# Feed-forward: early output products cut in three and written between the seven block products, TensorE in written order there, first such pair one later

## The chip, the cores and the metric

The kernel runs on one core of one Trainium2 chip. The metric is the device time of one execution in microseconds (us). Five engines matter here: TensorE (PE in the profile, with its weight loads as PEld), VectorE (DVE), ScalarE (ACT), GpSimd (POOL) and SyncE (SP), which only issues DMAs. Each engine works through its own instructions in one fixed order, and an instruction waits for semaphores that others raise.

## The reference

Two layers, each a feed-forward block, a mixer (neighbourhood attention in the first, a bidirectional RWKV-7 in the second) and another feed-forward block, with a normalized residual after each: four feed-forward blocks in all. Only they are touched:

```
D_MODEL, SEQ, D_FF = 1024, 512, 2816

def swiglu(x, w_in, w_out):
    gate, up = jnp.split(x @ w_in, 2, axis=-1)
    return (jax.nn.silu(gate) * up) @ w_out
...
x = layer_norm(DN_ALPHA * x + 0.5 * swiglu(x, ffn_w_in[i, 0], ffn_w_out[i, 0]), ln_g[i, 0], ln_b[i, 0])
```

x has 512 tokens of 1024 channels, w_in 1024 x 5632 and w_out 2816 x 1024, all float32.

## The kernel before

**Numbers.** A float32 operand is held as two parts: a rounded high part, made by an activation on ACT (line 277), and the remainder, a subtraction on DVE (line 278). This pair of steps is called a split. A product of two such operands is three matmuls: high by high, high by low, low by high.

**Blocks.** The 2816 hidden channels are 22 blocks f of 128, taken as 11 pairs c (f = 2c and f = 2c + 1) in `ffn` (line 462). A *standard block* (`proj`, line 291) takes gate and up one after the other: 2 x 8 x 3 = 48 matmuls of 512 columns (lines 287 to 289). Gate goes to one PSUM bank and up to another. ACT takes the silu of gate (line 494) and DVE multiplies it with up (line 496). From f = 2 on, `Seven.banks` gives every block the same two banks, so a block can't start in a bank before the last block's readers are done with it.

**Seven products.** The odd blocks from f = 3 on (`SEVEN`, line 83) use a 2 x 2 block scheme with seven multiplications in place of eight (`Seven.products`, line 962). Each product is 12 matmuls of 256 columns (line 979), 84 in all. Names used below: a, f, e, a2, e2, f2, e3, in the written order of the seven calls of `mul`. a and f (and a2, f2) share the first bank, e, e2 and e3 have the second. After a, ACT copies it from the first bank into the second, `copy(e, a)` (line 985 calls the helper of line 971). This copy writes the bank from which line 496 reads the standard block's up, so it comes after line 496; and f, in the bank that the copy reads, comes after the copy. Lines 993 to 1002 turn the products into the two halves of the block's result: line 998 on DVE reads f2 from the first bank, line 1002 reads e3 from the second. `operands` (line 943) loads the two weight tiles (lines 948, 949), forms four sums and differences of half tiles on DVE (lines 953 to 957), and makes four splits: two full tiles (`units`), half a tile (`one`), and a full tile (`pair`). The sums of x that the scheme needs are made once per feed-forward block by `mixes` (line 912), in two parts at f = 0 and f = 1.

**Output products.** w_out is handled by a second seven-product scheme over the pair's two blocks, token halves and output halves (`Winograd`, line 1005). Three of its products, X, Y and Z, accumulate over the 11 pairs while the pairs are being made. `early(c)` (line 1037) issues them for pair c: 3 x 2 token tiles x 3 = 18 matmuls of 512 columns (line 1058), into six PSUM banks. With the two banks of the blocks these are all eight. `early(c - 1)` is called in pair c, after its standard block. Its operands are `an`, a split of sums of the pair's results (lines 502 to 507), and three tiles `wx`, which `sums` (line 1014) makes: it loads 1 MB of w_out into the single buffer `ra` (line 1018), forms four differences on DVE (lines 1020 to 1023), writes two of them to DRAM (lines 1024, 1025) and splits three into `wx` (line 1029). `wx` has three buffers, so a split for pair c waits until the product of pair c - 1 that used the buffer has run, and `ra` is free for the next load when the third split is done.

**What sets the order.** A planner orders each engine's instructions when the kernel is built, by its own model of their times, with the written order as priority. Where a stretch stands under `manual_schedule(engines=...)`, the engines named there keep the written order. In the feed-forward blocks before the change nothing in the loop over pairs does. The four remaining output products (V, then lines 546, 551 and 564) follow the loop.

Of the kernel before, what the change touches and what calls it, by code (L numbers as in the profile page):

```python
# [22 lines left out]
NF = FF // P  # L23
# [26 lines left out]
MANUAL = {mybir.EngineType.PE}  # L50
# [29 lines left out]
EARLY_TAGS = ("kz1", "v", "vr", "qc", "qd", "zs", "qs", "tm")  # L80
DECAY = math.exp(-0.5)
GN_EPS = 64e-5
SEVEN = range(3, NF, 2)


A, B = slice(0, 64), slice(64, 128)
# [8 lines left out]
def halves_of(ap):  # L95
    return ap.rearrange("p (h t) -> p h t", h=2)
# [10 lines left out]
class Trunk:  # L107
# [20 lines left out]
    @contextmanager  # L128
    def early(self):

        with self.pool("ex", "right") as self.ex:
            self.turns = 0
            yield
        self.ex = None
# [327 lines left out]
    def ffn(self, xT, w_in, w_out, ln, nxt, lead=None):  # L462

        nc = self.nc
        npairs = NF // 2  # L470
        out = Winograd(self, w_out)
        seven = Seven(self, xT, w_in)
        with self.pool("fa") as pool:
            out.pool = pool
            keep = [self.ring().rearrange("p (c n i s) -> p c n i s", c=2, n=2, i=2) for _ in range(npairs // 2)]
            keep = [k[:, c] for k in keep for c in range(2)] + [seven.rest.rearrange("p (n i s) -> p n i s", n=2, i=2)]
            for c in range(npairs):
                with self.behind(*() if c or ln else (self.asked,)):
                    out.sums(c)
                raw = pool.tile([P, 8, 256], F32, name="ar", tag="ar", bufs=1)  # L480
                for j in range(2):
                    f = 2 * c + j
                    dst = raw[:, 3:7:3] if j else raw[:, 0:8:7]
                    if f == 0:
                        pps = self.follow()
                    elif f in SEVEN:
                        seven.products(f, dst)
                    elif not pps:
                        us = self.units if f == 1 else [self.load_cols(w_in, FF * i + f * P, eng=nc.vector) for i in range(2)]
                        pps = [self.proj(u, pp, xT) for u, pp in zip(us, seven.banks(f))]  # L490
                    if pps:
                        pg, pu = pps.pop(0), pps.pop(0)
                        s = self.tmp()
                        nc.scalar.activation(s, pg, AF.Silu)

                        nc.vector.scalar_tensor_tensor(dst, halves_of(pu), 0.5, halves_of(s), ALU.mult, ALU.mult)
                    if f < 2:
                        seven.mixes(f)
                    if j == 0 and c:
                        out.early(c - 1)  # L500
                a = lambda n: raw[:, n]
                nc.vector.tensor_tensor(a(1), a(7), a(6), ALU.add)
                nc.vector.tensor_tensor(a(2), a(1), a(0), ALU.subtract)
                nc.vector.tensor_tensor(a(4), a(0), a(7), ALU.subtract)
                nc.vector.tensor_tensor(a(5), a(3), a(2), ALU.subtract)
                out.now[c] = pool.tile([P, 2, 3, 256], F32R, name="an", tag="an", bufs=1)
                self.split(out.now[c][:, 0], out.now[c][:, 1], raw[:, 0:3])
                self.split(keep[c][:, :, 0], keep[c][:, :, 1], raw[:, 3:5])
                tag = ("gbc", "bbc")[c % 2]
                away = self.home(self.sb).tile([P, 2, 2, 256], F32R, name="away", tag=tag)  # L510
                self.split(away[:, :, 0], away[:, :, 1], raw[:, 5:7])
                nc.sync.dma_start(self.away[:, :, c], away.bitcast(F32).rearrange("p n i s -> p n (i s)"))
            params = self.ln_params(ln)
            out.keep = {n: [k[:, n] for k in keep] for n in range(2)}
            late = npairs - 4
            out.raws = self.pair(F32)
            out.add("V", 0, out.b21, range(0, late))
            out.early(npairs - 1)
            out.add("V", 0, out.b21, range(late, npairs))
        nxt = nxt()  # L520
        with self.pool("fo") as pool:
            out.pool = pool
            out.begin(out.t3)
            out.recall(2)
            fin = self.residual_norm(params, nxt)
            hs = (slice(0, 512), slice(512, 1024))

            def more(t, h, acc, scale=1.0, sm=None):
                y = self.x[t][:, hs[h]]
                nc.vector.scalar_tensor_tensor(y, y, scale, acc[t % 2], ALU.mult, ALU.add, accum_out=sm)  # L530

            X, Y, Z, V = (out.acc[n] for n in "XYZV")
            st = [self.small("st", 5) for _ in range(NT)]
            for t in (0, 1):
                more(t, 1, Y, ALPHA)
            for t in (2, 3):
                more(t, 1, Z, ALPHA)
            for t in (0, 1):
                more(t, 1, X)
            for t in (2, 3):  # L540
                more(t, 1, X)
                more(t, 0, X, ALPHA)
            for t in (0, 1):
                more(t, 0, X, ALPHA)
                more(t, 0, V, 1.0, st[t][0])
            out.add("Y", 1, out.t3, range(npairs))
            out.begin(out.b22)
            out.recall(3)
            for t in (2, 3):
                more(t, 1, Y, 1.0, st[t][1])  # L550
            out.add("Z", 2, out.b22, range(npairs), lag=8)
            out.begin(out.t4)

            def done(t):
                h, acc = (1, Z) if t < 2 else (0, Y)
                more(t, h, acc, 1.0, st[t][h])
                fin(t, st[t])

            done(0)
            done(1)  # L560
            mid = nxt and self.mark(self.x[1][:, 0:1])
            if isinstance(nxt, XT):
                out.raws = None
            out.add("Y", 3, out.t4, range(npairs), lag=6)
            if isinstance(nxt, XT):

                def start(t):
                    more(t, 0, Y, 1.0, st[t][0])
                    return fin(t, st[t], True)

                self.ending(start, lead, nxt, (mid,), (mid,))
            elif nxt:
                self.mid = mid
                with self.tc.manual_schedule(engines=MANUAL_SCAN):
                    self.fill = {3: 11}
                    more(2, 0, Y, 1.0, st[2][0])
                    n2 = fin(2, st[2], True)
                    for _ in range(3):
                        next(n2)
                    more(3, 0, Y, 1.0, st[3][0])  # L580
                    n3 = fin(3, st[3], True)
                    for n in (n3, n3, n3, n2, n3):
                        next(n)
            else:
                done(2)
                done(3)
        return nxt
# [302 lines left out]
class Seven:  # L890
# [68 lines left out]
        k.split(self.pair[:, 0], self.pair[:, 1], raws[0])  # L959
        return units  # L960

    def products(self, f, dst):

        k, nc = self.k, self.nc
        ua, ub = self.operands(f)
# [2 lines left out]
        a, f, e = a[:, :256], a[:, 256:], e[:, :256]  # L968
# [6 lines left out]
        def mul(out, w, x, start):  # L975
            for c in range(4):
                cs = slice(c * P, c * P + P)
                for n, (i, j) in enumerate(((0, 0), (0, 1), (1, 0))):
                    m = nc.tensor.matmul(out, w[:, i, cs], x[:, j, c], start=start and c + n == 0, stop=c == 3 and n == 2,  # L979
                                         skip_group_check=True)  # L980
                    if c + n == 0:
                        first.append(m.ins)

        b, t = self.block, self.right
        mul(a, ua[:, :, lo], b(0, 0), True)
        copy(e, a)
        with k.behind(first[0]):
            mul(f, ub[:, :, lo], t[0], False)
        copy(p, f)
# [8 lines left out]
        nc.vector.tensor_tensor(v[:, 0], f, v[:, 0], ALU.add)  # L998
        nc.scalar.activation(s[:, 1], v[:, 0], AF.Silu)
        nc.vector.scalar_tensor_tensor(dst[:, 1], v[:, 1], 0.5, s[:, 1], ALU.mult, ALU.mult)  # L1000
        mul(e, ub[:, :, hi], t[3], False)
        nc.vector.scalar_tensor_tensor(dst[:, 0], e, 0.5, s[:, 0], ALU.mult, ALU.mult)


class Winograd:
# [31 lines left out]
    def early(self, c):  # L1037

        a = self.now.pop(c)
        for name, n, u in zip("XYZ", (0, 2, 1), self.units.pop(c)):  # L1040
            first = self.banks(name)
            for t in range(2):
                self.product(self.acc[name][t], a[:, :, n], t, u, first, c == NF // 2 - 1)

    def recall(self, n):

# [985 lines left out]
```

## Time and profile before

| what | value |
|---|---|
| median of 3 runs | 2300.55 us (2291.13 to 2300.61) |
| the profiled execution | 2302.0 us |
| its span, first to last instruction | 2300.1 us |
| TensorE busy / instructions | 2147.4 us (93%) / 15392 matmuls |
| VectorE busy | 1581.6 us (69%) |
| ScalarE busy | 1101.9 us (48%) |
| mean granted TensorE clock | 0.978 |
| four loops over pairs | from about 18, 639, 1022 and 1928 us to 325, 943, 1321 and 2226 us |

A row of the chain of work or of the waits names the waiting instruction by engine, tile and line and, behind the arrow, what released it. A row of a timeline has start, duration (both us), engine, line, operation and tiles, how many were merged, and in brackets the idle time of the engine before it with what ended it. A row of a table of windows has, for each engine, busy time and in brackets the number of instructions. Matmuls overlap, so a matmul's duration is longer than the distance to the next one; the distance is what counts.

### The profile page before, as it was taken

The numbers are of one execution on the slowest core, as the hardware profiler recorded it, in microseconds if no ns is written. First come the engines' busy times: TensorE is split into PE (matmuls) and PEld (weight loads), VectorE is DVE, ScalarE is ACT, GpSimd is POOL, SyncE is SP. The second block draws the span as 40 slices with busy tenths as digits, with TensorE's granted clock in tenths as the row PEclk, the third lists the DMA queues.
The fourth block names the chain that finished last, engine by engine and source line by source line (L and its number), as shares of the span: only waits on it lengthen the run. The fifth ranks groups of instructions, "written<-read, shape, count | busy, mean of one in ns | idle before, by whom it ended". The sixth has DMA issues, their size and how long they took to land.

```text
span 2300.1 us, 39118 instructions
## 1 busy us (share of the span) xinstructions
PE 2147.4 (93%) x15392; PEld 1749.3 (76%) x15392; DVE 1581.6 (69%) x2542; ACT 1101.9 (48%) x2015; POOL 521.1 (23%) x670
## 2 busy tenths in 40 slices
PE   8899999999979999997999999999899999799998
PEld 7788788888878788886878887535666558688886
DVE  8676667277477677687666779835778558677766
ACT  4444444367344444454444453636677533444443
POOL 1000015464400000340000053044777610000014
PEclk9899999999989999999999999999999999999999
DMA  5444475342334444833444574764444551444464
GB/s 167 156 159 155 146 271 184 116 130 75 110 112 153 134 160 147 327 131 121 161 141 154 186 272 138 262 219 114 125 107 121 171 180 55 147 147 156 153 244 189
DMA packets 160809, 367.86 MB, mean 160 GB/s; under 512 B 32144, under 2 KB 52240, under 8 KB 158576
## 3 DMA queue, kind: packets, MB, share of 16 engines
q1 hardware_dynamic: 160624, 365.36, 48.1%
q8 instruction: 121, 1.98, 0.4%
q14 instruction: 64, 0.52, 0.1%
HBM read 284.29 MB, written 68.94 MB: 154 GB/s over the span
## 4 chain that ended last, share of the span: by engine, by line
PE 64%; DVE 15%; DMA 14%; ACT 3%; issue 3%; SPq 0%; DVEq 0%; ACTq 0%
PE bank L1058 15%; DMA ra<-in_ffn_w_out_dram 8%; PE bank L287 8%; PE bank L288 7%; PE bank L289 7%; PE a L1250 5%; PE bank L979 4%; PE bank L350 4%; DVE w L278 3%; DMA raw<-in_ffn_w_in_dram 3%; DVE wx L278 1%; DVE ring L278 1%; ACT w L277 1%; PE g L1574 1%; PE y L1250 1%
## 5 line engine op out<-in xcount | busy, mean ns | idle before, releaser
L278 POOL TENSOR_TENSOR w<-raw,w 128x1024 fp32r<-128x1024 f32 x38 | 93.4, 2463 | 1301.0 <-ACT w L277 1295.4
L287 PE MATMUL bank<-xT,w 128*128 128x512 f32 x704 | 285.1, 405 | 45.3 <-DVE tmp L998 45.2
L277 ACT ACTIVATE w<-raw 128x1024 fp32r<-128x1024 f32 x202 | 212.6, 1056 | 154.1 <-PE bank L979 82.3
L288 PE MATMUL bank<-xT,w 128*128 128x512 f32 x704 | 279.8, 397 | 0.0
L289 PE MATMUL bank<-xT,w 128*128 128x512 f32 x704 | 278.3, 396 | 0.0
L278 DVE TENSOR_TENSOR w<-raw,w 128x1024 fp32r<-128x1024 f32 x164 | 200.2, 1221 | 75.1 <-ACT w L277 75.1
L979 PE MATMUL bank<-ring,w 128*128 128x256 f32 x960 | 136.6, 293 | 66.6 <-ACT bank L971 66.6
L287 PEld LDWEIGHTS bank<-xT,w 128*128 128x128 f32 x704 | 134.9, 192 | 78.6 <-DVE tmp L998 51.8
L1058 PE MATMUL bank<-wx,an 128*128 128x512 f32 x792 | 188.2, 390 | 0.1
L979 PEld LDWEIGHTS bank<-ring,w 128*128 128x128 f32 x960 | 124.4, 197 | 75.6 <-ACT bank L971 75.6
L1058 PEld LDWEIGHTS bank<-wx,an 128*128 128x128 f32 x792 | 147.2, 188 | 30.4 <-DVE an L278 0.5
L1058 PE MATMUL bank<-w,ring 128*128 128x512 f32 x720 | 168.5, 390 | 0.0
L289 PEld LDWEIGHTS bank<-xT,w 128*128 128x128 f32 x704 | 135.4, 192 | 29.6
L1058 PEld LDWEIGHTS bank<-w,ring 128*128 128x128 f32 x720 | 134.9, 188 | 28.5
L1020 DVE TENSOR_TENSOR ts<-ra 128x512 f32<-128x512 f32 x44 | 30.4, 690 | 182.6 <-DMA ra<-in_ffn_w_out_dram 182.6
L288 PEld LDWEIGHTS bank<-xT,w 128*128 128x128 f32 x704 | 135.6, 193 | 26.4
L277 ACT ACTIVATE ring<-raw 128x512 fp32r<-128x512 f32 (+1 forms) x107 | 95.8, 900 | 101.8 <-DVE raw L956 71.8
L979 PE MATMUL bank<-ring 128*128 128x256 f32 x960 | 130.7, 286 | 0.0
L1681 POOL TENSOR_TENSOR tm<-qs,zs 128x126 f32<-128x126 f32 (+22 forms) x248 | 103.7, 418 | 88.0 <-issue 43.0
L979 PEld LDWEIGHTS bank<-ring 128*128 128x128 f32 x960 | 123.5, 196 | 0.1
L277 ACT ACTIVATE wx<-ra 128x512 fp32r<-128x512 f32 x132 | 81.5, 629 | 81.8 <-PE bank L1058 78.0
L278 DVE TENSOR_TENSOR wx<-ra,wx 128x512 fp32r<-128x512 f32 x132 | 96.9, 741 | 34.6 <-ACT wx L277 34.6
(383 smaller groups left out, 4764.7 us busy)
## 6 DMA issues: line engine op xcount, KB each, us to landing
raw<-in_ffn_w_in_dram SPq DMA_DIRECT2D x176, 512.0 KB, 4.2
ra<-in_ffn_w_out_dram SPq DMA_DIRECT2D x44, 1024.0 KB, 6.0
d_away<-away SPq DMA_DIRECT2D x44, 512.0 KB, 3.0
ring<-d_away SPq DMA_DIRECT2D x16, 1024.0 KB, 11.7
xT<-d_late SPq DMA_DIRECT2D x29, 512.0 KB, 8.5
xT<-in_ffn_w_out_dram SPq DMA_DIRECT2D x23, 512.0 KB, 8.2
d_late<-ts SPq DMA_DIRECT2D x44, 256.0 KB, 2.0
d_late<-ra SPq DMA_DIRECT2D x44, 256.0 KB, 2.0
```

What stands on the lines that cost most here:

```text
L277: self.hi = self.nc.scalar.activation(h, raw, AF.Copy).ins
L278: self.lo = (eng or self.nc.vector).tensor_tensor(l, raw, h.bitcast(F32), ALU.subtract).ins
L287: nc.tensor.matmul(out, wh, xh, start=start, stop=False)
L288: nc.tensor.matmul(out, wh, xl, start=False, stop=False)
L289: nc.tensor.matmul(out, wl, xh, start=False, stop=stop)
L350: nc.tensor.matmul(acc[t, h], a, u[:, i, h * 512 : (h + 1) * 512], start=first and n == 0, stop=last and n == 2)
L979: m = nc.tensor.matmul(out, w[:, i, cs], x[:, j, c], start=start and c + n == 0, stop=c == 3 and n == 2, skip_group_check=True)
L1020: nc.vector.tensor_tensor(t3, r[:, 1, 1], r[:, 0, 1], ALU.subtract)
L1058: self.nc.tensor.matmul(acc, lhs, u[:, i], start=bool(first) and m == 0, stop=last and m == 2, skip_group_check=more)
L1250: self.nc.tensor.matmul(out[hs], w[:, hs], x, start=start, stop=stop)
L1574: nc.tensor.matmul(pgs[h][:, j * P : (j + 1) * P], flat(bk[hs, q * 4 + j]), ar[hs, :, q * 4 + j], start=True, stop=True)
L1681: nc.gpsimd.tensor_tensor(tv, qs[:, s, 0:s].rearrange("p (a o) -> p a o", o=1).broadcast_to([P, s, n]), zs[:, s : s + 1, c0:].broadcast_to ...
```

## The change

The first block of seven products is f = 5 in place of f = 3; f = 3 becomes a standard block. `early` becomes a generator that stops after each of X, Y and Z. Where the pair's odd block is one of seven products, `early(c - 1)` is handed to `products`, which issues X behind product a, Y behind f2 and Z behind e3. Such a block's instructions are traced with TensorE in written order. For the pair of f = 2 and 3 the three products are issued together, as before.

```
-SEVEN = range(3, NF, 2)
+SEVEN = range(5, NF, 2)
...
                     elif f in SEVEN:
-                        seven.products(f, dst)
+                        with self.tc.manual_schedule(engines=MANUAL):
+                            seven.products(f, dst, out.early(c - 1))
...
-                    if j == 0 and c:
-                        out.early(c - 1)
+                    if c and f + 1 - j not in SEVEN and j == 0:
+                        list(out.early(c - 1))
...
-            out.early(npairs - 1)
+            list(out.early(npairs - 1))
...
-    def products(self, f, dst):
+    def products(self, f, dst, more):
...
         mul(a, ua[:, :, lo], b(0, 0), True)
         copy(e, a)
+        next(more)
         with k.behind(first[0]):
             mul(f, ub[:, :, lo], t[0], False)
...
         nc.vector.scalar_tensor_tensor(dst[:, 1], v[:, 1], 0.5, s[:, 1], ALU.mult, ALU.mult)
+        next(more)
         mul(e, ub[:, :, hi], t[3], False)
         nc.vector.scalar_tensor_tensor(dst[:, 0], e, 0.5, s[:, 0], ALU.mult, ALU.mult)
+        list(more)
...
                 self.product(self.acc[name][t], a[:, :, n], t, u, first, c == NF // 2 - 1)
+            yield
```

## The prediction

> **What bounds the kernel now.** I read the page first, then who waited for whom on TensorE, then TensorE's timeline through one feed-forward block, then a table of windows over all four.
>
> ```profile
> span 2300.1 us, 39118 instructions
> ...
> PE 64%; DVE 15%; DMA 14%; ACT 3%; issue 3%; SPq 0%; DVEq 0%; ACTq 0%
> ...
> ra<-in_ffn_w_out_dram SPq DMA_DIRECT2D x44, 1024.0 KB, 6.0
> ```
>
> ```profile
> PE bank L979 <- ACT bank L971: 66.6, 40, 11.3
> PE bank L287 <- DVE tmp L998: 45.2, 31, 3.3
> ```
>
> TensorE carries the chain. Its two largest waits, 111.8 us together, are both in the loop over pairs: once per block of seven products (40 times) product f waits for `copy(e, a)`, and 31 times the next standard block waits for line 998, which still reads the first bank. The change works on exactly these two.
>
> ```profile
> 71.67 0.40 PE L287 MATMUL bank<-xT,w 128*128 128x512 f32 x1
> ...
> 82.58 0.61 PE L1058 MATMUL bank<-wx,an 128*128 128x512 f32 x2
> ...
> 86.66 1.59 PE L979 MATMUL bank<-xT,w 128*128 128x256 f32 x12
> 88.88 1.69 PE L979 MATMUL bank<-ring,w 128*128 128x256 f32 x12 [0.63 <-ACT bank L971]
> ...
> 122.25 1.60 PE L979 MATMUL bank<-xT,w 128*128 128x256 f32 x12
> 123.69 1.60 PE L979 MATMUL bank<-ring 128*128 128x256 f32 x12
> ```
>
> These starts give TensorE's price of each piece. A standard block is 82.58 - 71.67 = 10.91 us, the 18 early matmuls 86.66 - 82.58 = 4.08 (so a third is 1.36), a product 123.69 - 122.25 = 1.44 and seven of them 10.08. A pair without any wait is 10.91 + 4.08 + 10.08 = 25.07 us. Seven products save only 0.83 us on a standard block, so one wait eats the saving.
>
> ```profile
> 45.99:71.67 25.68, 17.40 (x103) 15.81 (x102) 21.63 (x31) 11.47 (x18) 0.00 (x0) 0.80 0.46 155
> 662.20:689.90 27.70, 16.45 (x104) 15.38 (x103) 20.55 (x29) 10.55 (x18) 0.00 (x0) 0.75 0.44 145
> 1045.28:1072.67 27.39, 16.07 (x104) 15.00 (x102) 20.55 (x29) 10.54 (x18) 0.00 (x0) 0.81 0.46 148
> 1950.65:1977.49 26.84, 15.56 (x104) 14.49 (x102) 20.46 (x29) 10.58 (x18) 0.00 (x0) 0.81 0.49 150
> 71.67:324.67 253.00, 234.84 (x1352) 206.50 (x1351) 170.90 (x257) 109.67 (x171) 2.38 (x1) 0.98 0.46 154
> 689.90:943.13 253.23, 234.90 (x1353) 206.51 (x1351) 170.76 (x257) 109.57 (x171) 2.38 (x1) 0.98 0.47 155
> 1072.67:1321.06 248.39, 231.69 (x1353) 204.23 (x1352) 170.82 (x257) 109.99 (x171) 2.38 (x1) 0.99 0.47 157
> 1977.49:2226.09 248.60, 231.91 (x1353) 202.62 (x1352) 170.94 (x257) 110.10 (x171) 2.38 (x1) 0.99 0.47 158
> ```
>
> I cut each feed-forward block at two places. The first four rows run from the end of block f = 2 to the start of f = 4 and hold f = 3's seven products with the first early products: 107.61 us in all. The last four run from there to the start of V: nine pairs each, 1003.22 us in all, where 36 pairs without waits would be 36 x 25.07 = 902.5. So the nine-pair stretches lose 100.7 us, 2.80 per pair. In the fourth row DVE is busy 20.46 of 26.84 us, in the last 170.94/9 = 19.0 us per pair: the engine next in line.
>
> **Part 1, f = 3 as a standard block.** Without a wait the stretch is 4.08 + 10.91 = 14.99 us, four times 59.96; the most to gain is 107.61 - 59.96 = 47.7 us. What keeps f = 3 now?
>
> ```profile
> 57.94 0.68 DVE L957 TENSOR_TENSOR raw<-raw 128x512 f32<-128x512 f32 x1
> ...
> 58.55 0.68 DVE L278 TENSOR_TENSOR ring<-raw,ring 128x512 fp32r<-128x512 f32 x1
> ...
> 59.15 0.68 DVE L496 SCALAR_TENSOR_TENSOR ar<-bank,tmp 128x512 f32<-128x512 f32 x1
> ...
> 59.75 1.22 DVE L278 TENSOR_TENSOR ring<-raw,ring 128x1024 fp32r<-128x1024 f32 x1
> 59.86 0.37 ACT L971 ACTIVATE bank<-bank 128x256 f32<-128x256 f32 x1
> ...
> 60.28 1.01 PE L979 MATMUL bank<-ring,w 128*128 128x256 f32 x3 [8.15 <-ACT bank L971]
> ```
>
> ```profile
> 673.48 1.82 DVE L278 TENSOR_TENSOR ring<-raw,ring 128x512 fp32r<-128x512 f32 x2
> ...
> 676.81 0.68 DVE L496 SCALAR_TENSOR_TENSOR ar<-bank,tmp 128x512 f32<-128x512 f32 x1
> ```
>
> ```profile
> 1060.00 0.68 DVE L496 SCALAR_TENSOR_TENSOR ar<-bank,tmp 128x512 f32<-128x512 f32 x1
> ```
>
> ```profile
> 1965.40 0.68 DVE L496 SCALAR_TENSOR_TENSOR ar<-bank,tmp 128x512 f32<-128x512 f32 x1
> ```
>
> The wait is put down to ACT's copy, but the copy runs the moment line 496 of block f = 2 is done (59.15 + 0.68 = 59.83, copy at 59.86), and that sits in DVE's queue behind `mixes` and f = 3's operands. As a standard block, f = 3 needs line 496 only for its up half, which shares that bank. Its gate half (5.46) and the early products (4.08) come first, 9.54 us of cover: up may start at 55.5, 671.7, 1054.8 and 1960.2. DVE loses from ahead of line 496 the four half-tile steps and the `one` split, 0.605 each by starts (57.94, 58.55, 59.15), 3.0 in all, and in the later three also the `pair` split (59.75 to the next step, at most 1.22 by its duration), 4.2 together; the two weight splits stay. Line 496 then ends at 56.8, 673.3, 1056.5 and 1961.9: waits of 1.3, 1.6, 1.7 and 1.7, 6.3 in all. Part 1 gives 47.7 - 6.3 = 41.4 us. Its ends: 47.7 if the planner puts line 496 earlier, and, if DVE alone set the pace, about 4 x 4.2 = 17. I take 41.4, as DVE is idle about 7 of these 27 us (20.55 busy of 27.39), so it isn't the pace of the whole stretch. The loads are the same two of 512 KB per block, on the same queue.
>
> **Part 2, the nine pairs.** The copy: f started 88.88 - 86.66 - 1.44 = 0.78 us late with the copy prompt. X now stands in this gap with 1.36 us, 0.58 more than needed. X waits for `an` and `wx`; behind it in TensorE's fixed order stand f and everything else.
>
> ```profile
> 134.50 0.96 DVE L278 TENSOR_TENSOR an<-ar,an 128x768 fp32r<-128x768 f32 x1 [0.45 <-ACT an L277]
> ...
> 152.86 0.69 DVE L1020 TENSOR_TENSOR ts<-ra 128x512 f32<-128x512 f32 x1 [5.67 <-DMA ra<-in_ffn_w_out_dram]
> ...
> 155.55 0.41 DVE L998 TENSOR_TENSOR tmp<-bank,tmp 128x256 f32<-128x256 f32 x1
> ```
>
> ```profile
> 128.58:139.59 11.01, 11.01 (x48) 9.12 (x49) 9.41 (x15) 5.47 (x9) 0.00 (x0) 1.00 0.25 90
> ```
>
> `an` is ready at 135.46, in a standard block that runs to 139.59: X has over 5 us to spare. The other wait: line 998 is late because DVE stood 5.67 us waiting for `ra` with line 998 behind it. Y, e3 and Z now follow f2 before the next standard block: 1.36 + 1.44 + 1.36 = 4.16 us of cover for line 998 where there was 1.44. The longest wait so far was 3.3, of which 4.16 - 1.44 = 2.7 goes by this alone; and Z now ends behind all seven products, 10.08 us later than before, so its `wx` is released and `ra` asked for that much later, and DVE's stall for it leaves the seven products. I cost this wait at nothing.
>
> What is late next is DVE in the standard block, where it was busy 9.4 of 11.0 us.
>
> ```profile
> 128.25 1.06 ACT L277 ACTIVATE w<-raw 128x1024 fp32r<-128x1024 f32 x1 [2.54 <-PE bank L979]
> ...
> 129.53 0.62 ACT L277 ACTIVATE ring<-ar 128x512 fp32r<-128x512 f32 x1
> ```
>
> Into it move the four steps on `ra` (4 x 0.605 = 2.4) and DVE's part of two `wx` splits (0.68 each by the half-tile row above, 1.4). Out of it moves the weight split that starts when e3 frees its buffer (128.25): Z runs meanwhile, so its 1.2 us on DVE lie before the standard block. 9.4 + 2.4 + 1.4 - 1.2 = 12.0 us of work stand against 10.91, and line 496 comes about 1.1 late. The copy waits for it, f waits for the copy: 1.1 - 0.58 = 0.5 us. I add 0.2 for a copy queued behind a split on ACT and 0.4 for what is left of DVE's stalls on `ra`: 1.1 per pair, an estimate from these rows, with ends at 0 and at the 2.80 of now. Part 2 gives 100.7 - 36 x 1.1 = 61.1 us. On SP the later `ra` stands ahead of raw weight loads that are due a block later; their price is nothing.
>
> ```profile
> 239.21 0.50 PE L287 MATMUL bank<-xT,w 128*128 128x512 f32 x1 [1.65 <-DVE tmp L998]
> ...
> 250.23 1.07 PE L1058 MATMUL bank<-wx,an 128*128 128x512 f32 x4
> ```
>
> ```profile
> 267.23 0.73 PE L287 MATMUL bank<-xT,w 128*128 128x512 f32 x1 [1.97 <-DVE tmp L998]
> ...
> 279.86 0.40 PE L979 MATMUL bank<-xT,w 128*128 128x256 f32 x2
> ```
>
> One more price: after a pause of 1.65 us the standard block takes 250.23 - 239.21 = 11.02 us, after 1.97 it takes 12.63, 1.7 more than the 10.91. So a wait near 2 us costs almost twice itself, and 1.1 stays below that. The Trainium skill (TensorE: Matmul & The Clock Gate, Part 1) has the clock halve after an idle window of about 3.4 us; this trace shows a slow block after less, so the measurement decides. Were 2.0 us left per pair, the trace would make it 3.7 and the sum 2198 + 36 x 2.6 = 2292. By the page it would stay 2.0, and the sum 2231.
>
> **Sum.** 2302.0 (the profiled execution; its span and 1.9 us around it) - 41.4 - 61.1 = 2199.5. That execution was 1.45 above the median 2300.55, so against the median: 2198 us.
>
> **Rivals.** *Everything hidden:* the planner knows the new TensorE order and may put line 496 ahead of the steps on `ra`. For it: DVE has 25.07 - 19.0 = 6 us free per pair. Against it: line 1020 stood in DVE's queue up to 8.1 us before its data until now (row below). Time: 2302.0 - 1.45 - 47.7 - 100.7 = 2152.
>
> ```profile
> DVE ts L1020 <- DMA ra<-in_ffn_w_out_dram: 182.6, 36, 8.1
> ```
>
> *The DVE wait only moves:* stalled on `ra` in the standard block, DVE reaches line 496 so late that f loses what line 998 cost. Part 2 gives nothing, part 1 stays: 2302.0 - 1.45 - 41.4 = 2259. For it: `ra` takes 6.0 us from issue, so asked for 2 us after Z it lands 8 into the 10.91 us block, and 2.4 us of steps and some of the next operands stand behind it.
>
> *The same closed into a ring, slower than before:* Z ends, `wx` is split (1.3), `ra` loads, four steps (2.4), the operands behind them (4.2), line 496 and the copy (1.1), then f to Z (11.4). With 6.0 for the load it is 26.4 us, a loss of 1.3. With a load of 8, as the longest wait for it suggests, and the 1.7 of a slow block, it is 30.1: a loss of 5.0 per pair, 36 x (5.0 - 2.8) = 79 us more, 2259 + 79 = 2338. It decides from a loss of 2.80 + 41.4/36 = 3.95 us per pair. Against it: the median load is 6.0, and in the standard block DMA is busy only 0.25.
>
> *The clock drops with the smaller pieces:* X, Y and Z switch among six banks between products. Rows against it: six banks in turn gave 4.08 us for 18 now. If each pair paid one slow block, 36 x 1.7 = 61: 2198 + 61 = 2259. The Trainium skill (TensorE: Matmul & The Clock Gate, Part 1, the second failure mode) tells of the clock swinging when matmul groups cycle through banks.
>
> That the change doesn't do what it says, with TensorE's order as it was, I exclude: the written order is forced, and f = 3 leaves the scheme.
>
> **How the numbers follow.** The forecast has 0.50, everything hidden 0.20, the wait that only moves 0.18, the ring 0.07, the clock 0.05. The range 2152 to 2260 takes in the first three and the clock, 0.93, less misses at both ends of each. A measurement here can tell about 0.5%, 11.5 us, from no change. Faster by more than that: 0.50 + 0.20 + 0.05 and 0.14 of the third's 0.18, 0.89. The rest of the third, 0.04, with part 1 at its lower end and a little lost, is within it. Slower: the ring, 0.07.
>
> **What would show it.** Right: f = 3's stretch near 16.5 us in all four blocks; the wait of line 287 on line 998 gone; the wait of f on the copy about 1 us per pair and, followed back, on line 496; pairs near 26.2 us; DVE's wait for `ra` within the standard block and shorter than 182.6 us in all. Wrong: pairs at 27 us or more with f waiting for the copy; a wait in front of X, Y or Z; a slow standard block in most pairs; f = 5 inheriting f = 3's wait of 8 to 11 us.

## The result and the profile after

The changed kernel takes 2204.05 us (median of 4 runs, 2201.23 to 2208.95) against 2295.84 us for the kernel before (4 runs on the same chip): a ratio of 0.9603, 95% interval 0.957 to 0.9636. The forecast was 2198. The profiled execution of the changed kernel took 2204.32 us, 97.7 less than the profiled one before. Lines move: the copy's helper is now line 972, the seven products line 980, the early products line 1063, line 496 is 497, line 998 is 1000, and ra's four steps are lines 1024 to 1027. (In the kernel before, `copy(e, a)` is called in line 986; line 985 is product a.)

From the page of the changed kernel, the span, the engines' shares of the chain, and ra's transfers:

```profile
span 2201.7 us, 38797 instructions
...
PE 63%; DVE 18%; DMA 12%; ACT 3%; issue 2%; POOL 0%; SPq 0%; DVEq 0%; ACTq 0%; POOLq 0%
...
ra<-in_ffn_w_out_dram SPq DMA_DIRECT2D x44, 1024.0 KB, 5.2
```

TensorE's waits in the changed kernel (us in all, times, longest):

```profile
PE bank L980 <- ACT bank L972: 15.4, 26, 2.6
...
PE bank L1063 <- DVE w L278: 7.3, 4, 3.8
PE bank L287 <- DVE ar L497: 6.5, 7, 1.3
```

The wait for the copy fell from 66.6 to 15.4 us, the one for line 998 (45.2 us in 31) is gone. Two are new and small: line 497 in the start-up, as forecast, and a weight split in the output stage, which the forecast didn't have.

VectorE's own waits show what is left of the stall on ra, 182.6 us before:

```profile
DVE ts L1024 <- DMA ra<-in_ffn_w_out_dram: 86.8, 36, 4.0
```

To see where the time went, I cut each feed-forward block by the starts of TensorE's blocks: from the loop's start to the start of block f = 6, from there to V (eight pairs), and from V to the end of the output stage. (The prediction's cut at f = 4 can't be made in three of the four now, as the planner runs parts of f = 3, f = 4 and the early products through one another.) All four are summed here, for every kernel of this study, each from its own profiled execution:

| kernel | start to f = 6 | 32 pairs | per pair | V and after |
|---|---|---|---|---|
| before | 313.5 | 893.2 | 27.91 | 252.7 |
| changed | 274.8 | 820.3 | 25.63 | 264.6 |
| e1, seven products from f = 5 only | 274.5 | 880.9 | 27.53 | 259.0 |
| e2, three parts only | 309.0 | 820.1 | 25.63 | 262.5 |
| e3, planned order | 270.4 | 826.3 | 25.82 | 259.7 |
| e4, nothing behind a | 284.0 | 879.6 | 27.49 | 256.8 |
| e5, line 998 before ra's sums | 275.1 | 852.8 | 26.65 | 259.4 |
| e6, two parts behind a | 268.9 | 805.2 | 25.16 | 268.1 |
| e7, last pair as before | 277.6 | 826.1 | 25.82 | 259.2 |
| e8, mixes' splits on GpSimd | 324.9 | 880.6 | 27.52 | 253.2 |
| e9, ra's sums behind line 497 | 277.7 | 805.7 | 25.18 | 276.0 |
| e10, two parts behind f2 | 274.5 | 807.6 | 25.24 | 256.1 |

The change took 38.7 us from the start-up and 72.9 from the pairs, and gave 11.9 back in the output stage: 99.7 less in all, against 98.4 by the spans.

### The profile page after: what moved, and what is told of

It is laid out like the page before. It is cut to its first block, busy times and chain, and to the rows that moved or that the text cites. A ratio compares the mean times of both kernels' runs of the same rounds, so it can differ in the third digit from the quotient of the medians.

```text
span 2201.7 us, 38797 instructions
## 1 busy us (share of the span) xinstructions
PE 2131.1 (97%) x15248; PEld 1726.2 (78%) x15248; DVE 1551.5 (70%) x2506; ACT 1082.2 (49%) x1987; POOL 527.5 (24%) x670
## 4 chain that ended last, share of the span: by engine, by line
PE 63%; DVE 18%; DMA 12%; ACT 3%; issue 2%; POOL 0%; SPq 0%; DVEq 0%; ACTq 0%; POOLq 0%
PE bank L980 13%; PE bank L1063 12%; DMA ra<-in_ffn_w_out_dram 7%; PE a L1255 5%; PE bank L288 5%; PE bank L287 5%; PE bank L289 5%; DVE w L278 4%; PE bank L350 4%; DVE ring L278 2%; ACT w L277 2%; DMA raw<-in_ffn_w_in_dram 2%; PE g L1579 1%; PE y L1255 1%; DVE wx L278 1%
## 5 line engine op out<-in xcount | busy, mean ns | idle before, releaser
L287 PE MATMUL bank<-xT,w 128*128 128x512 f32 x760 | 298.1, 392 | 6.5 <-DVE ar L497 6.5
L288 PE MATMUL bank<-xT,w 128*128 128x512 f32 x760 | 296.1, 390 | 0.0
L289 PE MATMUL bank<-xT,w 128*128 128x512 f32 x760 | 295.7, 389 | 0.0
L1063 PE MATMUL bank<-wx,an 128*128 128x512 f32 x792 | 201.8, 392 | 0.0
L287 PEld LDWEIGHTS bank<-xT,w 128*128 128x128 f32 x760 | 142.7, 188 | 37.4 <-DVE ar L497 8.8
L289 PEld LDWEIGHTS bank<-xT,w 128*128 128x128 f32 x760 | 142.7, 188 | 30.0
L288 PEld LDWEIGHTS bank<-xT,w 128*128 128x128 f32 x760 | 142.8, 188 | 28.4
L980 PEld LDWEIGHTS bank<-ring,w 128*128 128x128 f32 x864 | 110.8, 191 | 33.4 <-ACT bank L972 30.4
L980 PE MATMUL bank<-ring,w 128*128 128x256 f32 x864 | 119.0, 287 | 15.7 <-ACT bank L972 15.4
L1688 POOL TENSOR_TENSOR zs<-zs,tm 128x126 f32<-128x126 f32 (+22 forms) x248 | 112.6, 454 | 19.4
L980 PE MATMUL bank<-ring 128*128 128x256 f32 x864 | 116.3, 284 | 0.1
L980 PEld LDWEIGHTS bank<-ring 128*128 128x128 f32 x864 | 109.6, 193 | 0.4 <-ACT tmp L972 0.4
L495 ACT ACTIVATE tmp<-bank 128x512 f32<-128x512 f32 x52 | 31.1, 597 | 151.8 <-PE bank L289 151.8
L980 PE MATMUL bank<-xT,w 128*128 128x256 f32 x756 | 100.6, 283 | 0.0
```

What stands on the lines that cost most here:

```text
L287: nc.tensor.matmul(out, wh, xh, start=start, stop=False)
L288: nc.tensor.matmul(out, wh, xl, start=False, stop=False)
L289: nc.tensor.matmul(out, wl, xh, start=False, stop=stop)
L1063: self.nc.tensor.matmul(acc, lhs, u[:, i], start=bool(first) and m == 0, stop=last and m == 2, skip_group_check=more)
L1688: nc.gpsimd.tensor_tensor(zs[:, 0:s, c0:], zs[:, 0:s, c0:], tv, ALU.add)
```

## The experiments

Theory 1 is the prediction's: two separate gains; X hides the copy, Y and Z hide line 998 as cover behind f2 and e3, and what is left of f's wait comes from VectorE having more work in the standard block than fits. The rivals came as runs spoke against its steps.

### One half of the change at a time

e1 is the kernel before, with one line changed. e2 is the changed kernel with this line as before.

```
-SEVEN = range(3, NF, 2)
+SEVEN = range(5, NF, 2)
```

> The kernel before with one edit, the seven products from f = 5. Theory (the two parts are separate; f = 3 waited for DVE's start-up queue, nothing else): from the start of a feed-forward block to the start of f = 6 it takes 4 x 72 = about 290 us in all four instead of 313.5, the later pairs stay at 27.9 us with both old waits, and the stage behind the loop stays as before. About 2260 us, ratio 0.985. Rival (the start-up queue only moves): f = 5 shows a wait of 8 to 11 us for its copy and the time stays within 0.5% of before, 2285 to 2300.

> The changed kernel with the seven products from f = 3 again, the three pieces and the written order kept. Theory: f = 3 waits 8 to 11 us for its copy as in the kernel before, the later pairs are at 25.6 us as in the changed kernel, and the stage behind the loop loses its 12 us. About 2204 + 30 = 2235 us, ratio 0.973. Rival (the pieces alone also mend f = 3, since X stands behind its product a): about 2205 us.

e1: 2251.86 us, 0.9819 of the kernel before (0.9779 to 0.9858). e2: 2231.4, 0.974 (0.9695 to 0.9785). Against the 2290.92 of the kernel before on this chip the two give 39 and 60 us, 99 together, where the whole change gives 91 to 92 (2295.84 - 2204.05). Each half does its own work: e1's start-up is that of the changed kernel to 0.3 us (274.5 and 274.8), e2's pairs are its pairs (25.63). Their sum is 7 to 8 us above the whole, which is no more than the two intervals allow; in the table e1 also takes 12.3 us from the pairs (893.2 to 880.9), and the whole change can't gain these twice.

### What made line 998 late: cover or its place in the queue

e3 lets the planner order TensorE's work in the seven products again; it puts all three parts behind a, so no cover stands behind f2 and e3. e4 keeps the written order and puts X behind f2, Y and Z behind e3.

```
 e3:
-with self.tc.manual_schedule(engines=MANUAL):
-    seven.products(f, dst, out.early(c - 1))
+seven.products(f, dst, out.early(c - 1))
 e4, in Seven.products:
         copy(e, a)
-        next(more)
```

> The changed kernel without the written order on TensorE. In the program that comes of it the planner puts all 18 early matmuls behind product a, and Y and Z no longer stand behind f2 and e3. Theory (Y and Z behind f2 are what hides line 998, and the late release of Z is what takes DVE's stall for ra out of the products): the wait of the next standard block for line 998 is back with 1 to 1.5 us per pair, f no longer waits, pairs at 26.5 to 27 us, about 2204 + 45 = 2249 us, ratio 0.98. Rival (only the copy behind product a cost time, and 4.08 us behind it hide it fully): pairs at 25.1, about 2190 us, ratio 0.954.

> The changed kernel with nothing behind product a: X behind f2, Y and Z behind e3, written order kept. Theory (X is worth its 1.36 us against the copy, and line 496, which the copy waits for, is about 1.9 us late in every pair): f waits 1.3 to 2 us per pair, pairs at 26.7 to 27 us, about 2204 + 45 = 2249 us. Rival (the bare copy of 0.78 us is all that X hid): pairs at 25.9, about 2204 + 10 = 2214 us.

e3: 2200.26 us, 0.9591 (0.9553 to 0.963). Theory 1 missed by 49 us: without the cover, the wait for line 998 is nearly gone all the same. TensorE's waits in e3 (line 999 there is line 998 of before):

```profile
PE bank L979 <- ACT tmp L971: 13.1, 9, 4.0
...
PE bank L287 <- DVE tmp L999: 5.2, 3, 2.3
```

e4: 2266.71, 0.9881 (0.9842 to 0.992), slower than both readings had it (2249 and 2214). It has the cover (Y and Z behind e3), but 27.49 us a pair. f waits for the copy 48.9 us in 36 again, so a part behind a is worth having; but a wait that neither reading had, of a2 for ACT's copy of f, adds 22.3 us in 27, and VectorE's weight splits wait for ACT 293.7 us where they waited 162.3 in the changed kernel. How much of the loss is the missing cover alone stays open. What e3 has and e1 hasn't shows on VectorE's timeline. First e1, a pair with a wait, then TensorE there:

```profile
807.16 0.69 DVE L1020 TENSOR_TENSOR ts<-ra 128x512 f32<-128x512 f32 x1 [1.12 <-DMA ra<-in_ffn_w_out_dram]
807.77 0.42 DVE L998 TENSOR_TENSOR tmp<-bank,tmp 128x256 f32<-128x256 f32 x1
```

```profile
808.24 0.50 PE L287 MATMUL bank<-xT,w 128*128 128x512 f32 x1 [0.85 <-DVE tmp L998]
```

Then e3:

```profile
754.46 0.42 DVE L999 TENSOR_TENSOR tmp<-bank,tmp 128x256 f32<-128x256 f32 x1
...
756.50 0.69 DVE L1023 TENSOR_TENSOR ts<-ra 128x512 f32<-128x512 f32 x1 [1.61 <-DMA ra<-in_ffn_w_out_dram]
```

In e1 the step that waits for ra's transfer stands ahead of line 998 in VectorE's queue, and line 998 waits with it, though f2 was long done. In e3 it stands behind. So the rival, theory 2: the place in VectorE's queue, not the cover, makes this wait. e5 tests it: e1, plus one dependence in VectorE's queue. The planner orders other steps anew with it, as it does with any change: in 29 of its 33 pairs the early products stand ahead of product a, while in 24 pairs of e1 six matmuls of a go first. But no product comes to stand behind f2 or e3 as cover.

```
-with self.behind(*() if c or ln else (self.asked,)):
+with self.behind(*(() if c or ln else (self.asked,)), *((self.read,) if c > 3 else ())):
     out.sums(c)
...
-nc.vector.tensor_tensor(v[:, 0], f, v[:, 0], ALU.add)
+k.read = nc.vector.tensor_tensor(v[:, 0], f, v[:, 0], ALU.add).ins
```

> The kernel of e1 (seven-product blocks from f=5, all 18 early matmuls in front of a, planner's order), and one more dependence: VectorE's four sums of ra for the next early product stand in its queue behind the line v0 = f + v0 of the pair, from the fourth pair on. TensorE's work and order, and the cover behind f2 and e3 (none), stay those of e1. Theory (place in VectorE's queue: a sum that waits for ra's transfer stood ahead of that line): the wait of the standard block on that line, 22.4 us in 15 waits in e1's profile, goes, with the slow standard blocks that follow a pause, up to 15 x 1.6 = 24 us; the copy's wait stays near 44 us in 33. Time 2252 - 22 to 46: about 2225, pairs near 26.4. Rival (cover: only matmuls between f2 and the standard block hide that line): the wait stays above 15 us and the time at 2245 to 2260. Second rival (the sums come too late for the early product): a new wait in front of the early matmuls, 2260 and more.

2227.49 us, 0.9712 (0.9674 to 0.975): theory 2, to 3 us. TensorE's waits in e1 and then in e5:

```profile
PE bank L979 <- ACT bank L971: 43.9, 33, 2.6
PE bank L287 <- DVE tmp L998: 22.4, 15, 3.2
```

```profile
PE bank L979 <- ACT bank L971: 35.9, 33, 2.1
PE bank L287 <- DVE tmp L998: 7.6, 4, 2.7
```

Some 24 us (0.0107 x 2296) came with one dependence that moves four steps in one queue, and without any cover. The four waits that are left are one in each feed-forward block. In the first block it is once more a step that waits ahead of line 998 in VectorE's queue, this time a weight split that waits for ACT:

```profile
169.67 1.23 DVE L278 TENSOR_TENSOR w<-raw,w 128x1024 fp32r<-128x1024 f32 x1 [6.52 <-ACT w L277]
171.19 0.42 DVE L998 TENSOR_TENSOR tmp<-bank,tmp 128x256 f32<-128x256 f32 x1
```

### What is left of f's wait

The changed kernel's pairs take 25.63 us; the prediction's sum without waits was 25.07. Theory 1 says VectorE is overfull and line 497 late. Line 497 is late: it starts 2.02 us behind the end of the standard block, that is, behind the start of TensorE's next matmul (median of the 32 pairs), against 0.20 before. Whether too much work makes it so, or again a wait, was open. e6 puts Y behind a too, and Z behind f2:

```
         copy(e, a)
         next(more)
+        next(more)
```

> The changed kernel with its three parts placed X and Y behind a, Z behind f2, nothing behind e3, all in written order. Theory (the sum of line 497 comes about 1 to 2 us late and the copy of f's bank waits for it; two parts behind a cover 2.8 us in place of 1.4): the waits of f on the copy, 15.4 us in 26 in the changed kernel's profile, fall below 6, pairs go from 25.6 to about 25.2, and as VectorE's queue has v0 = f + v0 ahead of ra's sums, less cover behind f2 costs nothing: 2204 - 32 x .4 = about 2190. Rival (cover behind f2 and e3 is what hides v0 = f + v0): a wait of the standard block on that line comes back, 0.5 us or more per pair, and pairs stay at 25.6 or go above: 2204 to 2225.

2183.54 us, 0.9528 (0.9499 to 0.9557), by the ratios some 17 us less than the changed kernel (0.0075 x 2296); 25.16 us a pair. But in e6 line 497 starts 0.20 us behind the block, so that more cover for the copy wasn't what helped, or not alone: something had taken VectorE's delay away (Z, too, stands one product earlier in e6). Here is VectorE in a pair of the changed kernel, then ACT and TensorE:

```profile
731.86 0.68 DVE L278 TENSOR_TENSOR wx<-ra,wx 128x512 fp32r<-128x512 f32 x1
...
737.85 0.69 DVE L1024 TENSOR_TENSOR ts<-ra 128x512 f32<-128x512 f32 x1 [2.63 <-DMA ra<-in_ffn_w_out_dram]
...
743.21 0.68 DVE L497 SCALAR_TENSOR_TENSOR ar<-bank,tmp 128x512 f32<-128x512 f32 x1
```

```profile
743.99 0.37 ACT L972 ACTIVATE bank<-bank 128x256 f32<-128x256 f32 x1 [0.80 <-DVE ar L497]
```

```profile
741.04 1.60 PE L980 MATMUL bank<-xT,w 128*128 128x256 f32 x12
742.47 1.55 PE L1063 MATMUL bank<-wx,an 128*128 128x512 f32 x6
744.40 1.70 PE L980 MATMUL bank<-ring,w 128*128 128x256 f32 x12 [0.38 <-ACT bank L972]
```

The third split of wx waits for Z's matmuls; when it is done, ra's only buffer is free and the next load starts; 6.0 us after that split began (737.85 - 731.86) VectorE gets on, having stood 2.63 us with line 497 behind it. Theory 3: this ring, closed by Z's place behind e3, makes line 497 late. Two runs tell it from cover and from work. e9 leaves TensorE's order alone and puts ra's four steps behind line 497 in VectorE's queue; this takes both the wait and the steps' own 2.4 us from ahead of line 497, so it speaks against cover, not against work. e10 moves Z alone, one product earlier, and leaves the work where it is.

```
 e9 (fetch is the load of ra, cut out of sums):
-    out.sums(c)
+    out.fetch(c)
+    if c < 3:
+        out.sums(c)
...
+    up = nc.vector.scalar_tensor_tensor(dst, halves_of(pu), 0.5, ...)
+    if c > 2:
+        with self.behind(up.ins):
+            out.sums(c)
 e10:
         nc.vector.scalar_tensor_tensor(dst[:, 1], ...)
         next(more)
+        next(more)
         mul(e, ub[:, :, hi], t[3], False)
```

> The changed kernel, TensorE's order as there (X behind a, Y behind f2, Z behind e3); ra's transfer is asked for at its old place, but from the fourth pair on VectorE's four sums of ra stand in its queue behind line 497 of the same pair. Theory (in the changed kernel line 497 starts 2.1 us behind the standard block because VectorE stood 2.4 us a pair waiting for ra ahead of it; the cover of one part behind a is enough): line 497 starts within 0.5 us, the waits of f on the copy fall from 15.4 us to below 5, pairs go from 25.6 to about 25.1, and the time to 2204 - 32 x .5 = about 2188. Rival (one part behind a does not cover the copy, whatever line 497 does): waits of 0.2 to 0.5 us a pair stay, pairs at 25.5, time 2198 to 2206.

> The changed kernel with X behind a, Y and Z both behind f2, nothing behind e3. Theory (a ring: Z's matmuls free the wx buffer that the next pair's last split waits for, and with that ra's only buffer, its transfer, VectorE's sums and line 497; Z one product earlier, about 1.4 us, ends VectorE's wait for ra from 2.4 us a pair to about 1): line 497 comes 1 us earlier or more, f's waits fall below 8 us, pairs to 25.1 to 25.3, time 2188 to 2195. Rival (cover behind a alone sets f's wait; Z's place plays no part): waits as in the changed kernel, pairs 25.5 to 25.6, time 2200 to 2206. The sum v0 = f + v0 has two parts and a product behind it in either case.

e9: line 497 starts 0.20 us behind the block, f's wait goes from the pairs (7.2 us in 3 are left, one at the start of each of three feed-forward blocks), and the pairs take 25.18 us, as theory 3 says. The total, 2200.36 us (0.9584, 0.9545 to 0.9624), doesn't: what the pairs gain, 14.6 us, the output stage takes back with 11.4 (264.6 to 276.0). It answers the question on the pairs and misses on the time.

e10: 2181.82 us, 0.9516 (0.9484 to 0.9548): with e6 the fastest, faster than the changed kernel by 0.0087, some 20 us, and the intervals don't touch. That is below the 2188 to 2195 expected: by the table the pairs give 12.7 us, about as expected, and the output stage happens to give another 8.5 (264.6 to 256.1). X alone stands behind a, as in the changed kernel, and it is enough. VectorE in a pair of e10:

```profile
723.47 0.69 DVE L278 TENSOR_TENSOR wx<-ra,wx 128x512 fp32r<-128x512 f32 x1 [0.33 <-ACT wx L277]
...
729.45 0.69 DVE L1025 TENSOR_TENSOR ts<-ra 128x512 f32<-128x512 f32 x1 [0.64 <-DMA ra<-in_ffn_w_out_dram]
...
735.72 0.68 DVE L497 SCALAR_TENSOR_TENSOR ar<-bank,tmp 128x512 f32<-128x512 f32 x1
```

Again 6.0 us from the split to ra's first step, but the split now begins 0.57 us before the standard block (724.04), where it began 1.70 after it (730.16) in the changed kernel. VectorE's wait for ra over the whole kernel falls from 86.8 to 21.1 us. And VectorE isn't overfull. The standard blocks of these two pairs, the changed kernel and then e10 (third figure: VectorE busy):

```profile
730.16:741.04 10.88, 10.88 (x49) 9.01 (x48) 8.25 (x12) 3.90 (x7) 0.00 (x0) 1.00 0.49 169
```

```profile
724.04:734.95 10.91, 10.91 (x50) 9.02 (x49) 10.12 (x16) 4.53 (x7) 0.00 (x0) 1.00 0.50 178
```

With 10.12 us of work done in the block line 497 follows 0.8 us behind it; with 8.25 it follows 2.2 behind. Over the 32 pairs VectorE works 10.5 us from the start of the standard block to line 497 in the changed kernel and stands 2.4; in e10 it works 11.0 and stands 0.55 (medians). It was the wait.

### The 12 us of the output stage

e7 gives the last pair of each feed-forward block the order of before.

```
-seven.products(f, dst, out.early(c - 1))
+seven.products(f, dst, out.early(c - 1) if c < npairs - 1 else iter(()))
...
-if c and f + 1 - j not in SEVEN and j == 0:
+if c and (f + 1 - j not in SEVEN or c == npairs - 1) and j == 0:
```

> The changed kernel, with the early matmuls of the last pair of each feed-forward put behind its standard block, as in the kernel before; the other pairs as changed. Theory (the 12 us that the output stages gained come from the last pair, whose written order lets the output stage's weight splits and sums fall into VectorE's queue later): the four output stages fall from 61.5, 62.0, 60.1 and 80.9 to what e1 shows (61.4, 61.5, 60.6, 75.5) or below, the wait of line 1063 on w from 7.3 us to near nothing, and the four last pairs take 1 to 2 us more each: about 2204 - 6 + 6 = 2204, between 2198 and 2210. Rival (the output stages are longer because the pairs before are shorter, so that transfers and splits have less time in all): they stay at 264 us in sum, and the last pairs' loss stands alone: 2208 to 2212.

2207.53 us, 0.9629 (0.9601 to 0.9657), not to be told from the changed kernel. The output stages fall to 259.2, as expected and close to e1's 259.0, and the pairs give it back. Of the 11.9 us, e1, which has no three parts, shows 6.3 and e2, which has nothing else, 9.8: the two don't add up. And e10 keeps the last pair in written order and has 256.1, so the written last pair as such isn't the cause. The place is clear: the changed kernel's fourth output stage, VectorE, GpSimd and then TensorE:

```profile
2131.97 6.06 DVE L531 SCALAR_TENSOR_TENSOR x<-x,bank 128x512 f32<-128x512 f32 x10
2137.95 2.88 DVE L278 TENSOR_TENSOR wl<-held,wl 128x1024 fp32r<-128x1024 f32 x1
2140.75 0.68 DVE L531 SCALAR_TENSOR_TENSOR x<-x,bank 128x512 f32<-128x512 f32 x1
2141.35 2.23 DVE L278 TENSOR_TENSOR w<-held,w 128x512 fp32r<-128x512 f32 x1
```

```profile
2137.34 2.40 POOL L278 TENSOR_TENSOR w<-held,w 128x1024 fp32r<-128x1024 f32 x1 [6.38 <-ACT w L277]
2140.20 2.84 POOL L278 TENSOR_TENSOR w<-xT,w 128x1024 fp32r<-128x1024 f32 x1 [0.45 <-ACT w L277]
```

```profile
2130.41 9.46 PE L1063 MATMUL bank<-w,ring 128*128 128x512 f32 x40
2143.64 6.32 PE L1063 MATMUL bank<-w,ring 128*128 128x512 f32 x14 [3.77 <-DVE w L278]
```

One split, half a tile, stands behind ten evictions and another split; TensorE waits 3.77 us for it and then runs 14 matmuls in 6.32 us, at a granted clock of 0.50, where 40 took 9.46 before. Both of VectorE's splits are long because GpSimd splits beside them: the first takes 2.88 us and 1.21 in e10, where GpSimd stands still at that moment, the second 2.23 where a half-tile split alone takes 0.69 (in e10 the second alone meets GpSimd, and takes 2.81). By these rows some 3.2 of the 3.77 us are this meeting, an estimate that no run tried. The wait is 3.8 us at its longest in the changed kernel and in e6, 0.6 in e10. Each kernel gets another order of these few steps from the planner, and with it other meetings; why this one here stays open.

### The start-up

f = 3's wait before was put down to VectorE's queue, full of the mixes' work. e8 takes one step of each mix off VectorE, in the kernel before.

```
-k.split(self.right[n][:, 0], self.right[n][:, 1], t)
+k.split(self.right[n][:, 0], self.right[n][:, 1], t, nc.gpsimd)
```

> The kernel before (seven-product blocks from f=3), with one step of each of the four mixes made at the start of a feed-forward, the remainder that splits its right operand, moved from VectorE to GpSimd. Theory (f=3's wait at the start is VectorE's queue: line 496 stands behind the mixes' steps): f=3's wait of 8 to 11 us shortens by the moved steps' time, 4 to 5 us in each feed-forward, and the stretch from the loop's start to f=6 falls from 313.5 us in four to near 296: about 2291 - 18 = 2273. Rival (f=3's data come late for transfers or for GpSimd's own splits): no change or worse, 2288 to 2310.

2304.8 us, 1.006 (1.0035 to 1.0085): slower, and the stretch is 324.9 us where 296 was expected. The same two steps of line 926 in the second feed-forward block, before and then in e8, with GpSimd's splits in e8 last:

```profile
648.69 1.22 DVE L926 TENSOR_TENSOR mixed<-xT,mixed 128x1024 f32<-128x1024 f32 x1
...
655.36 1.22 DVE L926 TENSOR_TENSOR mixed<-xT,mixed 128x1024 f32<-128x1024 f32 x1
```

```profile
647.40 3.00 DVE L926 TENSOR_TENSOR mixed<-xT,mixed 128x1024 f32<-128x1024 f32 x1
...
654.74 3.41 DVE L926 TENSOR_TENSOR mixed<-xT,mixed 128x1024 f32<-128x1024 f32 x1
```

```profile
646.92 2.40 POOL L278 TENSOR_TENSOR ring<-mixed,ring 128x1024 fp32r<-128x1024 f32 x1 [15.48 <-ACT ring L277]
...
653.65 3.41 POOL L278 TENSOR_TENSOR ring<-mixed,ring 128x1024 fp32r<-128x1024 f32 x1 [4.33 <-ACT ring L277]
```

The step that runs while GpSimd splits takes 3.0 to 3.4 us in place of 1.22: what GpSimd took over, VectorE lost again, and more: with 16 steps fewer its busy time in the whole kernel rose from 1581.6 to 1594.2 us. So e8 doesn't test what it was made for. That VectorE's queue held f = 3 rests on the trace of before alone.

## Why the prediction was right, and where its steps were not

**Part 1.** Forecast 41.4 us; e1, which is this part alone, gives 39 in the start-up (313.5 to 274.5). It also gives 39 by the medians, but that the two agree is partly chance, as e1's pairs gained 12.3 and its output stages lost 6.3. In the first feed-forward block, where the cut at f = 4 can still be made, f = 3's stretch is 16.58 us (46.21 to 62.79), forecast "near 16.5". The standard block's wait for line 497 was forecast as 1.3 to 1.7 us, 6.3 in all; the longest is 1.3, and all are 6.5. f = 5 inherited 2.3 to 2.6 us of f = 3's wait in three of the four, not 8 to 11.

**Part 2.** Forecast 1.70 us off each of 36 pairs; over the 32 that can be cut it is 2.28, since 25.63 us a pair is 0.56 above the sum without waits, not the 1.1 I allowed. f's wait for the copy was put at 0.5 a pair; f starts 3.22 us behind the standard block (median), 2.82 in e9 without the wait, so it is 0.40. Another 0.1 is that the three parts take 1.39 us each among products, where the sum had 1.36. The 0.2 for ACT and the 0.4 for stalls on ra, added separately, had next to nothing behind them: the stall on ra is itself the cause of f's wait, and I counted it twice. (A slip beside the sum: 2198 + 36 x 0.9 is 2230, not 2231.)

**A step that failed though its number held:** "1.36 + 1.44 + 1.36 = 4.16 us of cover for line 998 where there was 1.44", and so "I cost this wait at nothing." The wait went, but it goes without the cover too: e3 has none and 5.2 us of wait, e5 has none and 7.6. In the changed kernel itself the cover isn't used. Here line 998, now line 1000, reads f2's result; f2 ends where Y begins:

```profile
726.46 0.42 DVE L1000 TENSOR_TENSOR tmp<-bank,tmp 128x256 f32<-128x256 f32 x1
```

```profile
725.95 1.55 PE L1063 MATMUL bank<-wx,an 128*128 128x512 f32 x6
727.34 1.60 PE L980 MATMUL bank<-ring,w 128*128 128x256 f32 x12
```

The line is done 0.93 us after f2, and in 35 of the 36 pairs within 1.4 us, so that e3's 1.44 would hide it alone, as it stood before. The prediction had the true cause in the same passage, "line 998 is late because DVE stood 5.67 us waiting for `ra` with line 998 behind it", and that with Z's later end this stall "leaves the seven products". By e5 that is enough.

**A step that failed:** "12.0 us of work stand against 10.91, and line 496 comes about 1.1 late." It comes 2.0 late, and from a wait of 2.4 us a pair (86.8 / 36) for ra, not from work: e10 does the work of 11.0 us ahead of it, and line 497 comes 0.51 behind. So the mechanism was that of the rival called a ring, in its mild form. Its links (Z, the split of wx, the load, ra's steps, line 496, the copy, f) are those of the trace; its price was sized wrong, because it took a load of 8 us and a slow block each pair. The load took 5.2, and 32 of the standard blocks behind seven products took 10.88 to 11.06 us. With 5.2 in place of 6.0 that rival's sum without a slow block, 26.4, is 25.6, the pair that was measured. It was priced at its worst end, and given 0.07.

**Missed in the sum:** the output stage, 11.9 us dearer. In the table's cut the forecast was 41.4 + 4 x 1.70 = 48.2 us off the start-up and 32 x 1.70 = 54.4 off the later pairs. It came to 38.7 and 72.9: 9.5 less than forecast, 18.5 more, and 11.9 lost behind them, which the sum didn't have at all. These three errors all but cancel (2.9 us are left), so that 2198 lies within 6 us of 2204 is in part luck. The clock didn't drop with the smaller pieces: a part between two products takes 1.39 us (725.95 to 727.34 above), where it was 1.36, and the mean granted clock is 0.991, where it was 0.978.

## What to carry to other kernels

Where an engine waits, look in its own queue for what stands ahead of the step that is late: a step that waits for a transfer holds up everything behind it, and moving it one place (e5, 24 us) or freeing its buffer one product sooner (e10, 13 us in the pairs) can be worth as much as covering work. A single buffer that is freed by the last of several consumers makes a ring; follow it once around before choosing where the last consumer goes. A new order of one stage is paid for or refunded in the next by how the planner's order falls out there (256 to 276 us for the same output stage), so compare all stages, not the one that was changed.

## What the runs showed of the hardware

A pause of TensorE doesn't set the speed of the next block by its length alone. These are standard blocks in e1; TensorE had stood 3.19, 2.02, 2.10 and 2.50 us before them:

```profile
119.88:130.93 11.05, 11.05 (x48) 9.12 (x49) 9.69 (x16) 4.21 (x7) 0.00 (x0) 1.00 0.17 64
177.91:188.92 11.01, 11.01 (x48) 9.12 (x49) 9.69 (x16) 4.21 (x7) 0.00 (x0) 1.00 0.18 67
261.12:273.76 12.64, 12.64 (x48) 10.26 (x49) 9.32 (x15) 4.96 (x8) 0.00 (x0) 0.86 0.21 76
1954.38:1967.15 12.77, 12.77 (x49) 10.31 (x50) 10.18 (x17) 4.25 (x7) 0.00 (x0) 0.87 0.11 41
```

The granted clock stays at 1.00 after 3.19 us and falls to 0.86 after 2.10. The prediction read a bound between 1.65 and 1.97 us from two blocks; there is none. What counts is where a pause falls. In each of the twelve traces the stretches at half clock last 3.41 us or a multiple of it (the last one is cut off by the kernel's end), and they begin on one grid of 3.41 us. These are windows of that grid in e1 (first figure behind the length: TensorE busy; third from the end: granted clock):

```profile
114.64:118.05 3.41, 2.05 (x18) 1.85 (x16) 1.32 (x2) 1.06 (x1) 0.00 (x0) 1.00 0.03 12
118.05:121.46 3.41, 1.58 (x7) 1.30 (x8) 3.41 (x7) 0.97 (x2) 0.00 (x0) 1.00 0.73 221
145.36:148.77 3.41, 1.58 (x11) 1.33 (x11) 3.41 (x7) 1.61 (x3) 0.00 (x0) 1.00 0.52 99
148.77:152.18 3.41, 3.41 (x9) 2.64 (x8) 2.76 (x6) 0.41 (x1) 0.00 (x0) 0.50 0.54 191
258.00:261.41 3.41, 1.31 (x10) 1.10 (x9) 3.41 (x7) 1.36 (x2) 0.00 (x0) 1.00 0.52 117
261.41:264.82 3.41, 3.41 (x9) 2.65 (x9) 2.77 (x5) 0.66 (x2) 0.00 (x0) 0.50 0.55 191
```

The pause of 3.19 us is cut at 118.05 into 1.36 and 1.83, and the clock stays; the 2.10 us lie in one window, and the next one runs at 0.50. In these twelve traces a window at full clock in which TensorE stood 1.92 us or more was always followed by one at half clock, one with 1.76 us or less never; in between it went either way, as with the 1.83 us of the second and the third row. The Trainium skill (TensorE: Matmul & The Clock Gate, Part 1) calls the window in which activity is judged free-running; these rows agree. Its figure of about 3.4 us of idling for half the clock they don't bear out: 2.10 us lowered it.

A VectorE step with two inputs in SBUF takes 3.0 to 3.4 us beside a GpSimd split, 1.22 without (e8), and ends 1.1 us after GpSimd's split (650.40 and 649.32, 658.15 and 657.06), as if it had begun only then. The Trainium skill (SBUF — State Buffer, SBUF: two separate sides) has the two engines share a pair of ports, held by one of them for a whole instruction; the rows agree.
